# Bias rows in a box of their own, grouped queries read out before the merge, and layer 1's differential keys turned first, in a two-layer mixer trunk

## The chip, the cores and the metric

The kernel runs on one core of one Trainium2 chip. The metric is the device time of one execution in microseconds (us), the median of several runs. TensorE is called PE here, VectorE DVE, ScalarE ACT, GpSimd POOL and SyncE SP, as the profile does.

## The reference

Two layers act on 256 latent and 256 context tokens of width 1024. In each layer one normalised, modulated input h goes through four parallel mixers (a gated linear recurrence, differential attention, grouped-query attention, neighbourhood attention). Each mixer's output is multiplied by its own branch weight, scaled by a sigmoid gate and summed; then come an output projection and a feed-forward block. Context tokens go through the mixers of layer 0 only; in layer 1 they serve as keys and values. Cut to what this change touches:

```
(a_x, a_g, d_q, d_k, d_v, g_q, g_k, g_v, n_q, n_k, n_v, gates) = split_columns(h @ w_in + b_in)
y_b = rms_norm(softmax(q1 k1) v - lam * softmax(q2 k2) v)      # differential, 4 heads, rotary on q and k
y_c = gqa_attend(rope(rms_norm(g_q)), rope(rms_norm(g_k)), g_v)  # 4 query heads, 2 key heads
m = 0
for j, y in enumerate((y_a, y_b, y_c, y_d)):
    m = m + sigmoid(gates[j]) * (y @ w_branch[j])
out = m @ w_out + b_out
```

## The kernel before

Every matmul of full precision is three passes (`mm3`, L243 to L246): a weight tile is loaded by SP into one of two `raw` boxes (L185), ACT casts its high part `wh` (L214), DVE or POOL subtracts to get the low part `wl` (L217), and PE multiplies high by high, high by low, low by high. The passes accumulate in PSUM banks. The pool `mm` has three banks, `s` and `t` two each, `o` one.

`mixer` (L585) writes the work of a layer in this order: the recurrence (`lru`), the gates of branch 0, the differential branch up to its values (`diff` until its first `yield`), `merge(0)`, then differential attention and the gates of branch 1, then `gqa` until its first `yield`, `merge(1)`, the rest of `gqa` with the gates of branch 2, the start of `na`, `merge(2)`, and so on. A scheduler of the framework lays this program order out on the engines when the kernel is built: it may let independent work pass on each engine, and the order of each engine is then fixed. An engine runs its instructions in that order and waits where an operand is not there.

`merge(j)` (L660) takes the eight 128-wide slices of the model width in turn. For each slice PE does 6 matmuls of the branch output `y` with the branch weight into one `mm` bank, DVE multiplies the bank by the gate (`mt`, or `macc` for branch 0; L688), and for branches 1 and 2 POOL adds the product to `macc` (L691). In layer 0 a slice is 512 tokens wide, in layer 1 it is 256 wide.

`E` (L135) hands out six boxes of 128 x 516, shared by all short-lived tiles: the turned halves `dp` of the differential queries and keys, `dx` and `dt` beside them, the exponentials `e`, `mt`, the read-out queries `gx`, and the bias rows. `bias_row` (L578) takes such a box and asks for 256 bias values, spread over all 128 partitions, with a DMA on POOL's queue. It is called when the projection that needs it is written: in `v_proj` (L849) for the values of `diff` and `na`, and in `gqa` (L1047) for queries and for keys and values. DVE then reads the PSUM bank, adds the bias row and frees the bank (L856, L1064, L1084).

In `gqa` the query projection fills one `mm` bank for each segment: two in layer 0 (context and latent), one in layer 1 (`qs`). The banks are read out only after the `yield`, which is after `merge(1)`.

In `diff` (L946) queries and keys are turned one after the other: DVE takes the bank (`dx`, L964), PE permutes (`pp`, L967), DVE does the rotary products and the split into `dp` (L969 to L971, L829), and SP copies the halves in 24 small DMAs (L976) into `qx` or `qk`, the operands of the scores (`sps`, L1024). In layer 1 the key projection was done ahead: its two banks (one `mm`, one `o`) are full when the layer begins. There a query slice goes to `qx` and a key slice to `qk`; in layer 0 it is the other way round. A score of one head map needs the three DMAs of its query slice and the three of its key slice.

`par` (L482) is a pool of two boxes with a layer's small parameters; `params(0)` and `params(1)` take one each.

Of the kernel before, what the change touches and what calls it, by code (L numbers as in the profile page):

```python
# [8 lines left out]
F32 = mybir.dt.float32  # L9
# [101 lines left out]
class Trunk:  # L111
# [367 lines left out]

    def params(self, l, rowt):  # L480
        nc, i = self.nc, self.i
        par = self.per.tile([128, R_END], F32, tag="par", name="par", bufs=2)  # L482
# [93 lines left out]
    def bias_row(self, l, c0):  # L576
        t = self.E("brow2")[:, 0:256]
        self.nc.gpsimd.dma_start(t, self.i["b_in"][l:l + 1, c0:c0 + 256].broadcast_to([128, 256]))  # L578
        return t
# [5 lines left out]
    def mixer(self, l, x, hT, pool, tags):  # L585
# [6 lines left out]
        self.w = w  # L592
        self.full = [(0, T)] if l == 0 else [(0, 256), (256, 512)]
# [255 lines left out]
    def v_proj(self, col):  # L849
        nc = self.nc  # L850
        v = self.v_tiles()
        br = self.bias_row(self.l, col)
        units = self.cols_tm(self.w, col)
        for seg in range(2):
            ps = self.tm_chunk(units, seg)
            nc.vector.tensor_tensor(out=v[:, 2 * seg:2 * seg + 2, :], in0=ps, in1=bc(br, 1, [128, 2, 256]), op=ALU.add)  # L856
        return v
# [91 lines left out]
    def diff(self):  # L949
# [9 lines left out]
        for dst, col, slices, scale, order in ((q, "d_q", self.own, 32 ** -0.5, (0, 0, 1)),  # L959
                                               (k, "d_k", self.full, 1.0, (0, 1, 0))):  # L960
# [17 lines left out]
        v = self.v_proj(COL["d_v"])  # L978
# [69 lines left out]
    def gqa(self):  # L1048
# [4 lines left out]
        brq = self.bias_row(self.l, COL["g_q"])  # L1053
        uq = self.cols_tm(self.w, COL["g_q"])
        qs = []
        for seg in self.segs():
            qs.append(self.tm_chunk(uq, seg))
            if seg == self.segs()[0]:
                self.first_tm = self.last_tm
        yield  # L1060
        xs = []
        for ps in qs:
            t = view(self.E("gx"), 2, 256)
            nc.vector.tensor_tensor(out=t, in0=ps, in1=bc(brq, 1, [128, 2, 256]), op=ALU.add)  # L1064
            xs.append(view(t.rearrange("p a b -> p (a b)"), 2, 4, 64))
        normed = self.qk_norm(self.segs(), xs, 4, 0)
# [9 lines left out]
        brk = self.bias_row(self.l, COL["g_kv"])  # L1076
# [75 lines left out]
    def na(self):  # L1152
# [3 lines left out]
        q = [(qb[:, h, 0], qb[:, h, 1]) for h in range(4)]  # L1156
        for isk, col, slices, scale in ((0, "n_q", self.own, 0.125), (1, "n_k", self.full, 1.0)):
# [45 lines left out]
        v = self.v_proj(COL["n_v"])  # L1203
# [141 lines left out]
    def run(self):  # L1345
# [10 lines left out]
        self.l = 0  # L1356
# [212 lines left out]
```

## Time and profile before

| what | us |
|---|---|
| median of 3 runs (1497.87 to 1501.22) | 1499.52 |
| the profiled execution | 1494.38 |
| its span in the profile | 1492.6 |
| PE busy in the span | 1399.7 (94%) |
| DVE busy | 916.8 (61%) |
| ACT busy | 733.2 (49%) |
| POOL busy | 257.5 (17%) |

The profiled execution lies 5.1 us under the median, and 1.8 us of it lie around the span. Times in the text are us from the span's start. A row of the timeline has its start, its duration, the engine, the line, the operation, the tile written and the tiles read, the shape, the count, and in square brackets how long the engine was idle before and what released it. Matmuls overlap in the pipeline, so PE's pace is read from one start to the next (0.23 us for a 512-column pass at the full clock), not from the duration. Layer 0's mixers run from about 85 to 480 us, layer 1's from about 957 to 1245 us.

### The profile page before, as it was taken

Reading aid. Unit: us, or ns where it says so; the run is one execution under the profiler, and the core shown is the slowest. Engines: PE = TensorE matmul, PEld = TensorE weight load, DVE = VectorE, ACT = ScalarE, POOL = GpSimd, SP = SyncE. Lnnn points to the kernel's source line nnn. Section 1 sums busy time; section 2 is a strip of 40 time slices with the busy share of each in tenths; the row PEclk is TensorE's granted clock in tenths of the full one; section 3 lists DMA queues with packets and bytes.
Section 4 is the critical chain, followed back from the end, with each engine's and each line's share of the span. In section 5 each row is a group of like instructions: output and inputs, shape, how many; then the busy total and the mean of one; then the engine's idle time right before and its main releaser. Section 6 shows DMA issues by size and latency. Waiting matters only on the chain.

```text
span 1492.6 us, 22269 instructions
## 1 busy us (share of the span) xinstructions
PE 1399.7 (94%) x8420; PEld 1167.9 (78%) x8420; DVE 916.8 (61%) x1711; ACT 733.2 (49%) x1257; POOL 257.5 (17%) x445
## 2 busy tenths in 40 slices
PE   5999998899999999999999999998899999699997
PEld 3788676766887778777778888887788987599986
DVE  5664763642643988554545436767767657688856
ACT  4572452243254456454454223582636365577743
POOL 1120001211422102212222000010011321043421
PEclk9999999999999999999999999998899999799999
DMA  9425515213623454444543332343443526355562
GB/s 347 145 86 158 160 50 181 79 57 112 219 64 122 177 181 163 145 141 167 170 167 130 141 141 85 125 166 104 151 132 113 179 92 219 114 191 175 193 232 107
DMA packets 149310, 219.42 MB, mean 147 GB/s; under 512 B 10023, under 2 KB 118915, under 8 KB 149203
## 3 DMA queue, kind: packets, MB, share of 16 engines
q1 hardware_dynamic: 146690, 213.26, 42.8%
q0 software_dynamic: 2512, 4.73, 1.2%
q8 instruction: 67, 1.10, 0.3%
q14 instruction: 41, 0.33, 0.1%
HBM read 208.75 MB, written 1.08 MB: 141 GB/s over the span
## 4 chain that ended last, share of the span: by engine, by line
PE 76%; DVE 7%; DMA 6%; ACT 5%; issue 3%; SPq 2%; POOL 0%; DVEq 0%; ACTq 0%; POOLq 0%
PE mm L244 18%; PE mm L245 17%; PE mm L246 17%; PE acc L245 4%; PE acc L246 4%; PE acc L244 4%; PE ops L893 3%; PE adaps L380 2%; PE tp L885 2%; DMA raw<-in_w_in_dram 2%; DVE wl L217 2%; ACT wh L214 1%; DMA raw<-in_w_out_dram 1%; DMA raw<-in_ffn_w_dram 1%; PE sps L913 1%
## 5 line engine op out<-in xcount | busy, mean ns | idle before, releaser
L244 PE MATMUL mm<-hh,wh 128*128 128x256 f32 (+1 forms) x1488 | 501.7, 340 | 7.5 <-ACT gate L650 2.9
L245 PE MATMUL mm<-hl,wh 128*128 128x256 f32 (+1 forms) x1488 | 498.4, 336 | 0.0
L246 PE MATMUL mm<-hh,wl 128*128 128x256 f32 (+1 forms) x1488 | 497.3, 335 | 0.0
L214 ACT CAST wh<-raw 128x1024 fp32r<-128x1024 f32 x253 | 262.9, 1048 | 343.7 <-PE mm L245 155.1
L217 DVE TENSOR_TENSOR wl<-raw,wh 128x1024 fp32r<-128x1024 f32 x232 | 292.6, 1270 | 212.2 <-ACT wh L214 211.8
L244 PEld LDWEIGHTS mm<-hh,wh 128*128 128x128 f32 x1488 | 284.6, 192 | 46.8 <-issue 8.6
L246 PEld LDWEIGHTS mm<-hh,wl 128*128 128x128 f32 x1488 | 285.1, 192 | 31.1 <-issue 3.3
L245 PEld LDWEIGHTS mm<-hl,wh 128*128 128x128 f32 x1488 | 285.7, 192 | 29.4 <-issue 3.5
L1334 DVE SCALAR_TENSOR_TENSOR cv<-up,par,cv 128x512 f32<-128x512 f32 (+1 forms) x176 | 134.3, 764 | 52.7 <-ACT cv L1331 37.4
L245 PE MATMUL acc<-wl,a 128*128 128x512 f32 x232 | 90.7, 391 | 0.8 <-POOL wl L217 0.8
L870 ACT ACTIVATE e<-sps,nm 128x512 f32<-128x512 f32 (+1 forms) x96 | 59.2, 618 | 63.7 <-DVE nm L869 59.4
L246 PE MATMUL acc<-wh,a 128*128 128x512 f32 x232 | 90.3, 390 | 0.0
L244 PE MATMUL acc<-wh,a 128*128 128x512 f32 x232 | 89.6, 390 | 0.0
L869 DVE TENSOR_REDUCE nm<-sps 128x1 f32<-128x512 f32 (+1 forms) x96 | 56.7, 599 | 53.5 <-PE sps L914 37.4
L1338 POOL TENSOR_TENSOR cv<-cv 128x512 f32<-128x512 f32 (+1 forms) x44 | 50.0, 1135 | 165.9 <-ACT cv L1337 165.8
L244 PE MATMUL mm<-wh,hh 128*128 128x256 f32 x240 | 68.9, 287 | 0.8 <-DVE mt L688 0.8
L245 PE MATMUL mm<-wl,hh 128*128 128x256 f32 x240 | 68.2, 284 | 0.0
L246 PE MATMUL mm<-wh,hl 128*128 128x256 f32 x240 | 68.1, 284 | 0.0
L217 POOL TENSOR_TENSOR wl<-raw,wh 128x1024 fp32r<-128x1024 f32 x21 | 50.5, 2404 | 98.5 <-ACT wh L214 98.5
L312 ACT ACTIVATE junk<-x,nmu 128x512 bf16<-128x512 f32 x44 | 31.7, 721 | 70.0 <-DVE nmu L304 33.5
L1331 ACT ACTIVATE cv<-mm,cb,par 128x512 f32<-128x512 f32 (+1 forms) x88 | 58.5, 665 | 0.0
L244 PE MATMUL mm<-yh,wh 128*128 128x512 f32 (+1 forms) x128 | 47.0, 371 | 12.2 <-DVE mt L688 7.3
(313 smaller groups left out, 2135.8 us busy)
## 6 DMA issues: line engine op xcount, KB each, us to landing
raw<-in_ffn_w_dram SPq DMA_DIRECT2D x66, 1024.0 KB
raw<-in_w_in_dram SPq DMA_DIRECT2D x52, 1024.0 KB
raw<-in_w_ada_dram SPq DMA_DIRECT2D x40, 1024.0 KB
raw<-in_w_branch_dram SPq DMA_DIRECT2D x8, 1024.0 KB
raw<-in_w_out_dram SPq DMA_DIRECT2D x8, 1024.0 KB
w<-in_w_ada_dram SPq DMA_DIRECT2D x4, 1024.0 KB
w<-in_w_ada_dram SPq DMA_DIRECT2D x8, 512.0 KB
qk<-dp SPq DMA_DIRECT2D x48, 64.0 KB
```

The source lines that it names most:

```text
L214: nc.scalar.copy(hi, src)
L217: eng.tensor_tensor(out=lo, in0=src, in1=hi.bitcast(F32), op=ALU.subtract)
L244: nc.tensor.matmul(out, lhsT=lh, rhs=rh, start=start, stop=False)
L245: nc.tensor.matmul(out, lhsT=lh, rhs=rl, start=False, stop=False)
L246: return nc.tensor.matmul(out, lhsT=ll, rhs=rh, start=False, stop=stop)
L312: nc.scalar.activation(self.junk, halves[n], AF.Square, bias=nmu, accum_out=q[n])
L869: nc.vector.tensor_reduce(out=nm, in_=s if fold is None else fold, op=ALU.max, axis=AX.X, negate=True)
L870: nc.scalar.activation(e, s, AF.Exp, bias=nm, accum_out=total)
L893: self.last_pv = nc.tensor.matmul(o[64 * hh:64 * hh + 64, cs], lhsT=v[:, kt, vcol(hh)], rhs=pts[hh][:, kt, :], start=kt == 0, stop=kt == n ...
L1331: nc.scalar.activation(cv, view(ps, 2, 256)[:, 0:nseg, :], AF.Identity, bias=self.cb[:, j:j + 1], scale=tap[1])
L1334: nc.vector.scalar_tensor_tensor(out=cv, in0=up[:, :, k:k + 256], scalar=tap[k], in1=cv, op0=ALU.mult, op1=ALU.add)
L1338: nc.gpsimd.tensor_tensor(out=conv[0], in0=conv[0], in1=conv[1], op=ALU.mult)
```

## The change

Bias rows of `diff` and `na` values and of `gqa` keys and values no longer take an `E` box. A layer's mixer takes a `par` box of its own (`self.brow`), and the three rows are asked for, one after the other into the same box, as soon as `diff`, `gqa` or `na` begins. In layer 0 that box is the one that `params(1)` later uses (`self.boxes`); in layer 1 it is the box that `params(0)` had. The query row of `gqa` stays in an `E` box (`own=False`). In `gqa` the query banks are read out (`gx`) before the `yield`. In `diff` of layer 1 the keys are turned ahead of the queries.

```diff
     def params(self, l, rowt):
-        par = self.per.tile([128, R_END], F32, tag="par", name="par", bufs=2)
+        par = self.boxes.pop() if self.boxes else self.par_box()
...
-    def bias_row(self, l, c0):
-        t = self.E("brow2")[:, 0:256]
+    def bias_row(self, l, c0, own=True):
+
+        t = self.brow if own else self.E("brow2")[:, 0:256]
         self.nc.gpsimd.dma_start(t, self.i["b_in"][l:l + 1, c0:c0 + 256].broadcast_to([128, 256]))
         return t
...
+        box = self.par_box()
+        self.brow = box[:, 0:256]
+        if l == 0:
+            self.boxes.append(box)
...
-    def v_proj(self, col):
+    def v_proj(self, col, br):
         v = self.v_tiles()
-        br = self.bias_row(self.l, col)
...
-        for dst, col, slices, scale, order in ((q, "d_q", self.own, 32 ** -0.5, (0, 0, 1)),
-                                               (k, "d_k", self.full, 1.0, (0, 1, 0))):
+        br = self.bias_row(self.l, COL["d_v"])
+        sides = ((q, "d_q", self.own, 32 ** -0.5, (0, 0, 1)), (k, "d_k", self.full, 1.0, (0, 1, 0)))
+        for dst, col, slices, scale, order in sides[::-1] if self.l else sides:
...
-        brq = self.bias_row(self.l, COL["g_q"])
+        brq = self.bias_row(self.l, COL["g_q"], False)
+        brk = self.bias_row(self.l, COL["g_kv"])
         uq = self.cols_tm(self.w, COL["g_q"])
-        qs = []
+        xs = []
         for seg in self.segs():
-            qs.append(self.tm_chunk(uq, seg))
+            ps = self.tm_chunk(uq, seg)
             if seg == self.segs()[0]:
                 self.first_tm = self.last_tm
-        yield
-        xs = []
-        for ps in qs:
             t = view(self.E("gx"), 2, 256)
             nc.vector.tensor_tensor(out=t, in0=ps, in1=bc(brq, 1, [128, 2, 256]), op=ALU.add)
             xs.append(view(t.rearrange("p a b -> p (a b)"), 2, 4, 64))
+        yield
```

DVE in layer 0 around `merge(1)`, before the change (`do`, `yl` end the differential branch, `mt` is the merge, `gx` the query read-out, `gy` the start of the query norm):

```order
L996 COPY vt<-dn_2169 128x512
L217 TENSOR_TENSOR wl<-raw,wh 128x1024
L1003 SCALAR_TENSOR_TENSOR do<-vt,dlam,nb 128x512
L217 TENSOR_TENSOR wl<-raw,wh 128x1024
L829 TENSOR_TENSOR yl<-do,yh 128x512
L383 TENSOR_TENSOR ada<-ada,adaps 128x256
L688 SCALAR_TENSOR_TENSOR mt<-gate,mm 128x512 x8
L1064 TENSOR_TENSOR gx<-mm,brow_2187 128x512 x2
L217 TENSOR_TENSOR wl<-raw,wh 128x1024 x2
L1129 TENSOR_TENSOR gy<-gx,nw 128x512
```

The same place on DVE after the change:

```order
L1004 COPY vt<-dn_2169 128x512
L1070 TENSOR_TENSOR gx<-mm,brow_2187 128x512
L217 TENSOR_TENSOR wl<-raw,wh 128x1024
L1070 TENSOR_TENSOR gx<-mm,brow_2187 128x512
L1011 SCALAR_TENSOR_TENSOR do<-vt,dlam,nb 128x512
L217 TENSOR_TENSOR wl<-raw,wh 128x1024
L837 TENSOR_TENSOR yl<-do,yh 128x512
L383 TENSOR_TENSOR ada<-ada,adaps 128x256
L696 SCALAR_TENSOR_TENSOR mt<-gate,mm 128x512 x8
L217 TENSOR_TENSOR wl<-raw,wh 128x1024
L1135 TENSOR_TENSOR gy<-gx,nw 128x512
```

Both read-outs moved from behind the eight `mt` to ahead of `do` and `yl`; the norm still follows the merge.

SP in layer 1 around the differential copies, before the change (the five loads are of the recurrence's gate, branch 0's gates, and the differential projections; the single load behind the `w_ada` load is the first quarter of branch 1's gates):

```order
L185 DMA raw<-in_w_in_dram 128x8x256 x5
L185 DMA raw<-in_w_branch_dram 128x2x1024
L185 DMA raw<-in_w_ada_dram 128x2x1024
L185 DMA raw<-in_w_in_dram 128x8x256
L976 DMA qx<-dp 32x256 x24
L976 DMA qk<-dp 32x512 x24
L185 DMA raw<-in_w_in_dram 128x8x256 x4
```

The same place on SP after the change:

```order
L185 DMA raw<-in_w_in_dram 128x8x256 x5
L185 DMA raw<-in_w_branch_dram 128x2x1024
L185 DMA raw<-in_w_ada_dram 128x2x1024
L984 DMA qk<-dp 32x512 x24
L984 DMA qx<-dp 32x256 x24
L185 DMA raw<-in_w_in_dram 128x8x256 x5
```

The key copies stand ahead of the query copies, and the load of the first quarter of branch 1's gates stands behind all 48 copies.

PE in layer 1 at the end of `merge(0)` (`mm<-yh`), before the change (`mm<-hh` are the gates of branch 1, in passes of three matmuls; between the two scores stand 6 matmuls of the merge and 21 of the gates):

```order
L246 MATMUL mm<-yh,wl 128x256
L1024 MATMUL sps<-qk,qx 128x512
L244 MATMUL mm<-yh,wh 128x256
L245 MATMUL mm<-yl,wh 128x256
L246 MATMUL mm<-yh,wl 128x256
L244 MATMUL mm<-yh,wh 128x256
L245 MATMUL mm<-yl,wh 128x256
L246 MATMUL mm<-yh,wl 128x256
L244 MATMUL mm<-hh,wh 128x256
```

The same place on PE after the change (`tp` are transposes of the exponentials, `ops` the products with the values):

```order
L246 MATMUL mm<-yh,wl 128x256
L1032 MATMUL sps<-qk,qx 128x512 x4
L892 MATMUL tp<-cst,e 128x128 x4
L1032 MATMUL sps<-qk,qx 128x512 x3
L892 MATMUL tp<-cst,e 128x128 x4
L1032 MATMUL sps<-qk,qx 128x512 x2
L892 MATMUL tp<-cst,e 128x128 x4
L900 MATMUL ops<-vt 64x256
L1032 MATMUL sps<-qk,qx 128x512 x2
L892 MATMUL tp<-cst,e 128x128 x4
L1032 MATMUL sps<-qk,qx 128x512
L900 MATMUL ops<-vt 64x256 x7
```

Between the merge and the twelfth score no matmul of the gates is left; 48 of them stood there before.

## Rows read from the trace of the kernel before

**Rows 1.** The page, part 1: busy time, share of the span, instructions.
```profile
PE 1399.7 (94%) x8420; PEld 1167.9 (78%) x8420; DVE 916.8 (61%) x1711; ACT 733.2 (49%) x1257; POOL 257.5 (17%) x445
```
**Rows 2.** Stretches: PE, PEld, DVE, ACT, POOL busy, granted PE clock, DMA share, GB/s.
```profile
253.70:275.30 21.60, 14.76 (x67) 8.78 (x66) 8.65 (x14) 2.78 (x4) 8.98 (x7) 1.00 0.29 98
376.70:389.10 12.40, 12.40 (x67) 9.57 (x66) 9.20 (x12) 3.05 (x4) 7.95 (x7) 1.00 0.77 233
1028.00:1043.70 15.70, 11.30 (x53) 9.27 (x52) 10.22 (x21) 2.28 (x3) 0.62 (x1) 0.69 0.35 83
1043.70:1068.50 24.80, 20.29 (x101) 15.03 (x100) 17.50 (x34) 16.06 (x35) 0.00 (x0) 0.78 0.44 131
1068.50:1093.30 24.80, 23.68 (x186) 21.59 (x185) 14.83 (x35) 12.88 (x25) 0.55 (x1) 1.00 0.50 164
```
**Rows 3.** Waits in 253.7 to 275.3: engine, line, releaser, us in total, times, longest.
```profile
PE mm L244 <- DVE mt L688: 5.6, 7, 0.9
```
**Rows 4.** Timeline of PE in layer 0's merge(1): one slice ends, the next begins.
```profile
256.93 0.40 PE L246 MATMUL mm<-yh,wl 128*128 128x512 f32 x1
258.11 0.50 PE L244 MATMUL mm<-yh,wh 128*128 128x512 f32 x1 [0.78 <-DVE mt L688]
```
**Rows 5.** Timeline of DVE at that merge's end: the last product, the read-outs.
```profile
274.61 0.69 DVE L688 SCALAR_TENSOR_TENSOR mt<-gate,mm 128x512 f32<-128x512 f32 x1 [1.82 <-PE mm L246]
275.21 1.28 DVE L1064 TENSOR_TENSOR gx<-mm,brow 128x512 f32<-128x512 f32 x2
```
**Rows 6.** Timeline of POOL: seven additions of layer 0's merge(2).
```profile
382.79 9.77 POOL L691 TENSOR_TENSOR macc<-macc,mt 128x512 f32<-128x512 f32 x7 [1.35 <-DVE mt L688]
```
**Rows 7.** Timeline of PE in layer 0's merge(0): a score waits for its copies.
```profile
151.13 0.36 PE L1024 MATMUL sps<-qx,qk 96*128 96x256 f32 x1 [1.78 <-DMA qx<-dp]
```
**Rows 8.** Timeline of SP in layer 0: key copies, then the next loads.
```profile
144.42 15.09 SPq L976 DMA_DIRECT2D qx<-dp  x24
159.60 1.18 SPq L185 DMA_DIRECT2D raw<-in_w_in_dram  x2
```
**Rows 9.** Timeline of POOL and DVE in layer 1's merge(0): the bias row and its readers.
```profile
1037.65 0.62 POOL L578 DMA_DIRECT2D brow<-in_b_in_dram  x1 [20.03 <-DVE macc L688]
...
1041.42 1.29 DVE L856 TENSOR_TENSOR vt<-mm,brow 128x512 f32<-128x512 f32 x2 [1.71 <-DMA brow<-in_b_in_dram]
```
**Rows 10.** Timeline of SP in layer 1: query copies, key copies, the loads behind them.
```profile
1020.09 15.66 SPq L976 DMA_DIRECT2D qx<-dp  x24
1035.86 15.32 SPq L976 DMA_DIRECT2D qk<-dp  x24
1051.28 1.18 SPq L185 DMA_DIRECT2D raw<-in_w_in_dram  x2
```
**Rows 11.** Timeline of DVE in layer 1, up to the first query half.
```profile
1016.95 0.96 DVE L813 SCALAR_TENSOR_TENSOR ge<-ge,lru 128x256 f32<-128x256 f32 x1
...
1018.83 0.41 DVE L815 TENSOR_TENSOR yl<-ge,yh 128x256 fp32r<-128x256 f32 x1
...
1020.05 0.42 DVE L829 TENSOR_TENSOR dp<-dx,dp 128x256 fp32r<-128x256 f32 x1
```
**Rows 12.** Timeline of PE in layer 1: scores, gate matmuls at either clock, the first products.
```profile
1041.21 0.63 PE L1024 MATMUL sps<-qk,qx 96*128 96x512 f32 x1
...
1046.45 0.41 PE L245 MATMUL mm<-hl,wh 128*128 128x256 f32 x1
1046.66 0.41 PE L246 MATMUL mm<-hh,wl 128*128 128x256 f32 x1
...
1050.28 0.28 PE L245 MATMUL mm<-hl,wh 128*128 128x256 f32 x1
1050.40 0.28 PE L246 MATMUL mm<-hh,wl 128*128 128x256 f32 x1
...
1051.60 0.63 PE L1024 MATMUL sps<-qk,qx 96*128 96x512 f32 x2
...
1065.20 3.34 PE L893 MATMUL ops<-vt 128*64 128x256 f32 x14
```

More of the change, by code (lines that the diff above doesn't have):

```diff
@@ L478, in setup, with par_box @@
         nc.scalar.activation(self.silu_c[:, :, 0:2], pc[:, 0:16].rearrange("p (s k) -> p k s", s=2), AF.Silu)
+    def par_box(self):
+        return self.per.tile([128, R_END], F32, tag="par", name="par", bufs=2)
     def params(self, l, rowt):
         nc, i = self.nc, self.i
-        par = self.per.tile([128, R_END], F32, tag="par", name="par", bufs=2)
+        par = self.boxes.pop() if self.boxes else self.par_box()
         q = nc.sync
@@ L977, in diff @@
                                           parts[order[r]][32 * g:32 * g + 32, ts].bitcast(F32))
-        v = self.v_proj(COL["d_v"])
+        v = self.v_proj(COL["d_v"], br)
         yield
@@ L1075, in gqa @@
         kb = view(self.X("gkk", F32R), 2, T)
-        brk = self.bias_row(self.l, COL["g_kv"])
         uk = self.cols_tm(self.w, COL["g_kv"])
@@ L1156, in na @@
         q = [(qb[:, h, 0], qb[:, h, 1]) for h in range(4)]
+        br = self.bias_row(self.l, COL["n_v"])
         for isk, col, slices, scale in ((0, "n_q", self.own, 0.125), (1, "n_k", self.full, 1.0)):
@@ L1202, in na @@
         prepare(0)
-        v = self.v_proj(COL["n_v"])
+        v = self.v_proj(COL["n_v"], br)
         if self.l:
@@ L1355, in run @@
                 x[seg].append(xt)
-        self.l = 0
+        self.l, self.boxes = 0, []
         self.pre, self.w = {}, i["w_in"][0]
```

## The prediction

> **What bounds the kernel now.** I read the page first, for the engine that has no slack: PE is busy 94% of the span, the next engine 61% [rows 1]. So an edit pays only where PE stands still or runs at its lower clock, and a microsecond taken out of such a place comes off the end, unless something behind it is late for another reason. Next I read each `merge` as a stretch, with PE's busy time, count and granted clock beside it, because the change aims at the three PSUM banks of `mm` that a merge shares with unread projections [rows 2]. Three places stand out.
>
> In layer 0, `merge(1)` takes 21.60 us with PE busy 14.76. `merge(2)` does the same 67 matmuls in 12.40 us, busy all the time, at the same clock 1.00 [rows 2]. The list of waits names the reason: PE waits seven times, 5.6 us in all, for DVE's `mt` [rows 3]. The timeline shows one such step: the last pass of a slice starts at 256.93, the next slice only at 258.11, after 0.78 of waiting [rows 4]. The two query banks are read at 275.21, behind the last `mt` at 274.61 [rows 5]. Until then the merge has one bank in place of three, and PE and DVE take turns.
>
> In layer 0, `merge(0)` has a wait of 1.78, but for a copy into `qx` and not for a bias row [rows 7]. In layer 1, `merge(0)` takes 15.70 us with PE busy 11.30 at a clock of 0.69 [rows 2]; POOL's bias request waits 20.03 for an `E` box, and the value banks are read at 1041.42, once it has landed [rows 9]. What stands behind it is the start of differential attention, fed by SP's copies.
>
> **Grouped queries read out early, layer 0.** What is removed is the bank shortage. The upper end is the difference to `merge(2)`: 21.60 - 12.40 = 9.2. The lower end is the listed waits alone, 5.6. I take the upper end first, because the rest of the difference (busy 14.76 against 12.40) is the pipeline filling again after each wait: the pass after it starts later than 0.23 apart from its neighbour. What is added: the two read-outs, 1.28 of DVE together [rows 5], stand ahead of `do` and `yl`, which the merge's second pass needs. A cover for one of them is likely, since a weight split stands between the two and the banks are full early; I charge 0.7, with 0 and 1.28 as ends. So 9.2 - 0.7 = **8.5 gained**, ends 5.6 - 1.28 = 4.3 and 9.2.
>
> Are DVE, POOL and the boxes fast enough for a slice in 12.40 / 8 = 1.55? DVE needs 0.69 per `mt` [rows 5]. POOL did seven additions in 9.77, 1.40 each [rows 6]. An `mt` box is held 0.69 + 1.40 = 2.1, so two boxes are enough; the `gx` tiles hold two of the six during the merge, four are left for `mt` and others. `merge(2)` runs with the same three engines and shows that it goes. Behind the merge the key-value projection, the query norm and the key norm begin where the last `mt` ends, on both kernels; they move forward with it and keep their own waits. The request for key-value bias no longer needs an `E` box, which may give back a little more there; nothing in the sum counts it.
>
> **Bias row, layer 0.** SP's order is unchanged there: the 24 `qx` copies end at 144.42 + 15.09 = 159.5, the loads of the next gates follow at 159.60 [rows 8]. An earlier bias row lets PE do merge matmuls before the scores rather than between them, and the gates behind are still as late as their loads. I take **0**. Ends: a gain of 1.78 if the wait of rows 7 vanishes, a loss of 1.55 if one merge slice is put ahead of scores that were ready.
>
> **Keys first and bias row, layer 1.** PE's part of `merge(0)` is 48 passes of 256 columns. At the full clock two such starts lie 0.12 apart, at the half clock 0.21 [rows 12]; 48 x 0.12 = 5.8. With the value banks read at once the merge should end about 8 us earlier, at 1036. That gain is not the branch's gain. Attention waits for 48 copies on SP, 15.66 + 15.32 in one row [rows 10], and the first batch starts when its first half is split on DVE, at 1020.05. Ahead of the first key half now stand two `ge` and two `yl` fewer (the starts of rows 11 lie 0.33 apart, one `ge` takes 0.88): 0.88 + 3 x 0.33 = 1.9, less some 0.2 for wider key operations. So both batches move **1.7 earlier**: the second from 1035.86 to 1034.1, the last copy from 1051.2 to 1049.5.
>
> Between the first score, 1041.21, and the fourth, 1051.60 [rows 12], there stood merge and gate matmuls, partly at the half clock. Now the scores stand one behind the other, limited by copies: the first some 5.4 us behind the second batch's start, as before (1041.21 - 1035.86), so at 1039.5; three copies of 0.65 for the next head map, 2 us, and waits of the exponentials put the fourth at 1042 to 1045, say 1044. The first products end 1068.5 - 1051.6 = 16.9 behind the fourth score [rows 2, 12]: 1061, which is 7.5 earlier. But the 48 gate matmuls that PE used as filling are still to do, and their first load is now asked for behind all copies, at 1049.6, where before it went ahead. From 1061 there follow the 24.8 us of the last stretch in rows 2 and 48 x 0.12 = 5.8 more: 1091.6, against 1093.3. **Gain 1.5.** Ends: 7.5 if the 48 find idle places on PE before 1061; a loss of 5.8 if attention comes no earlier and the filling is only moved.
>
> The trace shows PE half-clocked in just such places: 0.21 between starts at 1046.45, a clock of 0.69 in `merge(0)` and 0.78 behind it [rows 2, 12]. If the 48 gate matmuls all ran so, they would cost 48 x 0.09 = 4.3 more. (The Trainium skill, "TensorE: Matmul & The Clock Gate", section "HAM oscillation — how this bites in real kernels", speaks against this part of the change: a PE that idles for data between bursts drops to half its clock, and the next burst begins there. The rows agree; by it alone the layer's 1.5 gain would become a loss of 2.8.)
>
> **The rest.** `merge(1)` of layer 1 has one query segment, so two banks stay free either way, and the neighbourhood rows come earlier to a place where PE did not wait for them: 0 for both. The extra `par` boxes are memory, not time.
>
> Sum on the profiled execution: -8.5 + 0 - 1.5 = -10, so 1494.4 becomes 1484.4. That execution is 5.1 under the median; the same -10 on the median 1499.5 gives **1489.5**.
>
> **The rivals.**
>
> *Both merges pay in full.* Layer 1 gives its upper end, as PE's idle places between scores take the gate matmuls after all: -8.5 - 7.5 = -16, 1483.5. For it: PE is the bound and 4.4 us of the merge are idle. Against: the load behind the copies.
>
> *Layer 1's attention is starved.* Half clock alone: -8.5 - 1.5 + 4.3 = -5.7, 1493.8. Attention no earlier: -8.5 + 5.8 = -2.7, 1496.8. Both: +1.6, 1501. I take 1496.8. For it: the order with no filling between merge and twelfth score, and the clock rows. Against: key halves ready 1.7 earlier.
>
> *The copies slip: slower.* The wider key halves hold `E` boxes until their copies have landed. If the next half finds no box, SP stands for a landing and a turning: a landing took 1041.42 - 1038.27 = 3.1 on POOL's queue [rows 9], a turning from the last `ge` takes at least 1020.05 - 1016.95 = 3.1 [rows 11], together 6.2. Two such gaps among the four halves cost 12.4, three 18.6, and scores and gate load are late by as much. From a slip of 10 the kernel is slower than before; two gaps give -10 + 12.4 = +2.4, three +8.6; middle +5.5, **1505**. Against: in the kernel before the two batches lie 0.1 apart with the same six boxes [rows 10], and a bias row no longer takes one.
>
> *The merge keeps its cadence.* If `gx` and what else is in `E` leave `mt` one box, a slice takes 2.1 and a hand-over, some 2.2 in place of 2.4: 8 x 0.25 = 2 gained, with layer 1 -3.5, **1496**; with nothing gained 1498. Against: `merge(2)`, above.
>
> **How the numbers follow.** A measurement of this kernel can tell about 0.2%, 3 us, from no change. Forecast, 1486 to 1493.5: 0.52. Both in full, about 1483.5: 0.14. Starved attention, about 1496.8: 0.16, half of it within 0.2%. Copies slip, about 1505: 0.10, of it 0.08 slower and 0.02 within. Cadence kept, 1496 to 1498: 0.08, nearly all within. Faster: 0.52 + 0.14 + 0.08 + 0.01 = 0.75; within: 0.08 + 0.02 + 0.07 = 0.17; slower 0.08. The range 1482.5 to 1497.5 leaves out the slip, the far end of starvation and a corner of the full pay, about 0.18.
>
> **What would show it.** Layer 0's `merge(1)` should last 12 to 13.5 us, with PE's waits for `mt` gone and both `gx` ahead of the first `mt`; if the waits stay, the first step is wrong. The key-value projection should begin about 8.5 earlier and that lead should hold at layer 0's end. Scores of layer 0's differential branch should stand within 1.5 us of their old place. In layer 1, less the lead, SP should copy keys from about 1018.4 without gaps to 1049.5; `merge(0)` should last about 8 us; the fourth score should come near 1044, the first products near 1061, and the gates end at 1091.6. A PE that stands waiting with half clock beyond 1061, or SP with gaps between the batches, would make the layer's term wrong; a `merge(1)` of over 17 us would take the forecast out of its range.

## The result and the profile after

The changed kernel takes 1476.36 us (median of 4 runs, 1474.13 to 1479.34) against 1498.69 for the kernel before, measured beside it (4 runs, 1496.59 to 1501.22): a ratio of 0.985, 95% interval 0.9825 to 0.9875. That is 22 us, with 19 to 26 inside the interval. 1489.5 was predicted, a gain of 10, with a range that ended at 1482.5. The direction was right, the size less than half of what came. In the profiled executions the last instructions stand 20.3 us earlier.

Part 1 of the page after, with the columns of [rows 1]:

```profile
PE 1395.8 (95%) x8420; PEld 1166.2 (79%) x8420; DVE 917.3 (62%) x1711; ACT 731.9 (50%) x1257; POOL 259.5 (18%) x445
```

The counts are unchanged, so no work has gone. PE is busy 3.9 us less for the same 8420 matmuls; the other 16 us are time in which it stood still. To see where, I took stretches between the same landmarks of PE in both traces: from the first matmul of layer 0's `merge(1)` to that of its `merge(2)`, and from the end of layer 0's feed-forward block to the first matmul of layer 1's `merge(1)`. The columns are those of [rows 2]: the stretch, its length, busy time and count of PE, PEld, DVE, ACT and POOL, the granted clock (the share of the full clock that TensorE was given, 0.5 or 1.0 at any moment), DMA share and GB/s. Before:

```profile
253.80:376.80 123.00, 112.58 (x605) 84.74 (x605) 59.30 (x123) 44.01 (x88) 21.68 (x28) 0.97 0.29 99
932.00:1099.10 167.10, 149.64 (x1103) 134.05 (x1102) 115.93 (x241) 95.55 (x167) 10.16 (x11) 0.93 0.43 137
```

After:

```profile
256.00:366.90 110.90, 108.28 (x606) 83.86 (x605) 60.12 (x122) 43.60 (x87) 22.44 (x28) 0.98 0.33 110
921.50:1079.80 158.30, 146.00 (x1103) 130.28 (x1101) 115.27 (x241) 95.08 (x167) 11.35 (x11) 0.94 0.45 144
```

Below I call them **stretch A** (layer 0, grouped queries) and **stretch B** (layer 1, differential branch). A gives 12.1 us, B 8.8. The rest of the span loses 0.6: a start-up that was 1.9 longer in this execution, where nothing is changed, less 1.3 in small pieces. So both places are those of the prediction; A was forecast at 8.5, B at 1.5.

Inside A, `merge(1)`, the stretch that answers to the first line of [rows 2]:

```profile
256.00:268.40 12.40, 12.40 (x67) 9.39 (x66) 8.24 (x13) 1.72 (x3) 6.87 (x6) 1.00 0.51 170
```

It is as long as `merge(2)` was to the tenth, with PE busy throughout; the seven waits of [rows 3] are gone. DVE's timeline at its beginning (start, duration, engine, line, operation, tiles, shape, count, idle time before):

```profile
249.66 0.69 DVE L1070 TENSOR_TENSOR gx<-mm,brow 128x512 f32<-128x512 f32 x1 [2.90 <-PE mm L246]
...
256.20 0.68 DVE L1070 TENSOR_TENSOR gx<-mm,brow 128x512 f32<-128x512 f32 x1
...
258.60 0.69 DVE L837 TENSOR_TENSOR yl<-do,yh 128x512 fp32r<-128x512 f32 x1
...
260.75 1.88 DVE L696 SCALAR_TENSOR_TENSOR mt<-gate,mm 128x512 f32<-128x512 f32 x3 [1.14 <-PE mm L246]
```

One read-out fell into a pause of DVE, the other stands ahead of `do` and `yl` as foreseen. PE didn't wait for the `yl` at 258.60, because its order puts the high passes of three slices together there, which three banks allow:

```profile
259.40 0.85 PE L244 MATMUL mm<-yh,wh 128*128 128x512 f32 x3
260.09 0.40 PE L245 MATMUL mm<-yl,wh 128*128 128x512 f32 x1
```

Inside B, `merge(0)`, then the stretch up to the end of the first products (of the exponentials with the values, `ops`), then the gates of branch 1:

```profile
1016.20:1023.10 6.90, 6.90 (x52) 6.38 (x51) 6.17 (x17) 0.81 (x2) 0.62 (x1) 1.00 0.42 107
1023.10:1044.10 21.00, 15.47 (x45) 8.18 (x44) 15.65 (x34) 12.83 (x30) 0.00 (x0) 0.59 0.44 135
1044.10:1074.00 29.90, 29.90 (x242) 28.14 (x241) 20.06 (x39) 17.96 (x33) 0.55 (x1) 1.00 0.56 181
```

`merge(0)` takes 6.9 in place of 15.7, at clock 1.00 in place of 0.69. Behind it PE starves: 45 matmuls in 21 us, clock 0.59. Then it works without a gap for 29.9 us at 1.00. SP's copies and the load behind them, as in [rows 10]:

```profile
1004.58 15.56 SPq L984 DMA_DIRECT2D qk<-dp  x24
1020.32 15.94 SPq L984 DMA_DIRECT2D qx<-dp  x24
1036.30 13.63 SPq L185 DMA_DIRECT2D raw<-in_w_in_dram  x4
```

Counted from the begin of B, copies start at 83.1 in place of 88.1 and end at 114.7 in place of 119.2: 5.0 and 4.5 earlier, not 1.7.

### The profile page after: what moved, and what is told of

Same layout as the page of the kernel before. It is cut to its first block, busy times and chain, and to the rows that moved or that the text cites. A ratio compares the mean times of both kernels' runs of the same rounds, so it can differ in the third digit from the quotient of the medians.

```text
span 1472.3 us, 22271 instructions
## 1 busy us (share of the span) xinstructions
PE 1395.8 (95%) x8420; PEld 1166.2 (79%) x8420; DVE 917.3 (62%) x1711; ACT 731.9 (50%) x1257; POOL 259.5 (18%) x445
## 4 chain that ended last, share of the span: by engine, by line
PE 76%; DVE 8%; DMA 6%; ACT 5%; issue 3%; SPq 1%; POOL 0%; DVEq 0%; ACTq 0%; POOLq 0%
PE mm L244 18%; PE mm L245 17%; PE mm L246 17%; PE acc L245 4%; PE acc L246 4%; PE acc L244 4%; PE ops L900 3%; PE adaps L380 2%; PE tp L892 2%; DMA raw<-in_w_in_dram 2%; DVE wl L217 2%; ACT wh L214 1%; DMA raw<-in_w_ada_dram 1%; DMA raw<-in_ffn_w_dram 1%; PE sps L920 1%
## 5 line engine op out<-in xcount | busy, mean ns | idle before, releaser
L245 PEld LDWEIGHTS mm<-hl,wh 128*128 128x128 f32 x1488 | 285.1, 192 | 29.9 <-issue 4.0
L699 POOL TENSOR_TENSOR macc<-macc,mt 128x512 f32<-128x512 f32 (+1 forms) x32 | 36.1, 1159 | 104.6 <-DVE mt L696 104.6
```

Source lines behind the costliest of these rows:

```text
L245: nc.tensor.matmul(out, lhsT=lh, rhs=rl, start=False, stop=False)
L699: nc.gpsimd.tensor_tensor(out=self.macc[n], in0=self.macc[n], in1=dst, op=ALU.add)
```

## Experiments

Each kernel was timed beside the kernel before; ratios are to that, with 95% intervals, and can differ by some tenths of a per cent from the quotient of the medians. A and B vary by some 1 us between two profiles: the changed kernel, profiled twice, showed 110.9 and 109.5 for A, 158.3 and 158.5 for B. B holds the same matmuls, by tile and shape, in all versions. Other stretches vary more, as the end of this document says.

### The read-out alone

```diff
-        qs = []
+        xs = []
         for seg in self.segs():
-            qs.append(self.tm_chunk(uq, seg))
+            ps = self.tm_chunk(uq, seg)
...
-        yield
-        xs = []
-        for ps in qs:
             t = view(self.E("gx"), 2, 256)
...
             xs.append(view(t.rearrange("p a b -> p (a b)"), 2, 4, 64))
+        yield
```

> The kernel before with one part of the change: the grouped queries' banks are read out ahead of merge(1); bias rows stay in E, layer 1 turns queries first. Theory 1 (the bank shortage is all of layer 0's gain): layer 0's merge(1) falls from 21.6 to 12.4-13 us, the lead behind layer 0's mixers is the 12 us that the full change shows there (median about -12, 1487). Rival (the read-out gives only the merge, and the 3 us behind it come from the key-value bias row in its own box): merge(1) as above, but the lead at layer 0's end is 8 to 9 (median 1490 to 1491). Layer 1 as before in both, its merge(0) 15.7 us.

Measured: 0.9922 (0.9892 to 0.9953), median 1484.56. Stretches A and B:

```profile
253.30:365.30 112.00, 108.36 (x606) 83.87 (x605) 60.23 (x122) 43.45 (x87) 22.44 (x28) 0.98 0.33 109
922.10:1089.50 167.40, 149.30 (x1103) 133.43 (x1102) 116.22 (x241) 94.94 (x167) 10.25 (x11) 0.93 0.43 136
```

A loses 11.0 of its 123.0 by this part alone, B nothing (167.4 against 167.1). Theory 1 holds in the main: the bank shortage is layer 0's gain. All kernels with the read-out have 109.5 to 112.2 in A, all without it 121.9 to 123.0. The two with the read-out and the key-value row still in `E` are the longest, 112.0 and 112.2, the eight profiles with the box 109.5 to 111.1, so the rival's share is about 1 us. PE's waits in A behind the merge show it: without the box PE waits three times before the scores (1.9, 0.6 and 1.2 here), with it twice (1.4 and 1.2).

### Keys first alone, and the box alone

The first has these lines of the change and nothing else:

```diff
-        for dst, col, slices, scale, order in ((q, "d_q", self.own, 32 ** -0.5, (0, 0, 1)),
-                                               (k, "d_k", self.full, 1.0, (0, 1, 0))):
+        sides = ((q, "d_q", self.own, 32 ** -0.5, (0, 0, 1)), (k, "d_k", self.full, 1.0, (0, 1, 0)))
+        for dst, col, slices, scale, order in sides[::-1] if self.l else sides:
```

The second has everything except those lines and the read-out, that is, of the change:

```diff
+        box = self.par_box()
+        self.brow = box[:, 0:256]
...
-        t = self.E("brow2")[:, 0:256]
+        t = self.brow if own else self.E("brow2")[:, 0:256]
...
+        br = self.bias_row(self.l, COL["d_v"])
...
+        brk = self.bias_row(self.l, COL["g_kv"])
...
+        br = self.bias_row(self.l, COL["n_v"])
```

> The kernel before with one part of the change: layer 1 turns the differential keys first; bias rows in E, query banks read out behind the merge. Theory 1 (layer 1's gain comes from the copies: keys lie ready in their banks, so the first turn needn't wait for the layer's own query projection): SP's copies start about 5 us earlier against the layer's start, and most of the 8.8 us of layer 1 is gained by this part alone, 6 to 8 us (median about 1492). Rival (layer 1's gain comes from the value banks, read at once): the copies start earlier, but merge(0) stays at 12 us or more, the scores stand behind it, and the gain is 0 to 2 us (median 1497 to 1499).

> The kernel before with one part of the change: bias rows of values, and of grouped keys and values, in their own box and asked for when the branch begins; the query banks are read out behind merge(1), layer 1 turns queries first. Theory 1 (copies decide in layer 1): layer 1's merge(0) falls from 15.7 to about 8 us, the scores come no earlier since the copies end as before, and layer 1 gains 0 to 2; layer 0 gains 0 to 1, so the median is about 1497 to 1499. Rival (value banks decide): layer 1 gains 6 to 8 by this part alone, median 1490 to 1493. If the bias row gives layer 0 the 3 us behind merge(1), another 3 less.

Measured, keys first: 0.9961 (0.9939 to 0.9983), median 1489.5 of ten runs from 1487.22 to 1496.09; stretch B, its `merge(0)`, and the request for the value row:

```profile
928.40:1089.10 160.70, 144.06 (x1102) 129.87 (x1101) 115.41 (x241) 94.50 (x167) 11.35 (x11) 0.96 0.44 142
1029.20:1039.00 9.80, 7.37 (x53) 6.32 (x51) 5.79 (x13) 1.92 (x5) 0.62 (x1) 1.00 0.28 67
```

```profile
1030.35 0.62 POOL L578 DMA_DIRECT2D brow<-in_b_in_dram  x1 [15.58 <-DVE dp L829]
```

Measured, the box: 0.9934 (0.9914 to 0.9953), median 1486.88; stretch B, its `merge(0)`, SP in its layer 1, and the fourth score on PE:

```profile
933.20:1094.20 161.00, 144.78 (x1103) 129.54 (x1102) 116.56 (x241) 95.55 (x167) 10.15 (x11) 0.96 0.44 142
1029.20:1040.40 11.20, 7.79 (x54) 6.64 (x53) 9.66 (x21) 2.29 (x3) 0.62 (x1) 1.00 0.26 65
```

```profile
1021.40 15.20 SPq L984 DMA_DIRECT2D qx<-dp  x24
1036.71 16.66 SPq L984 DMA_DIRECT2D qk<-dp  x24
```

```profile
1046.61 0.39 PE L1032 MATMUL sps<-qk,qx 96*128 96x512 f32 x1
```

Either part alone shortens B, by 6.4 and by 6.1; together they give 8.8, so for a good part they remove the same loss. With keys first the value row still takes an `E` box, but it is asked for 1.1 us behind the begin of `merge(0)`, against 9.7 before the change [rows 9], and both parts alone have `merge(0)` at a clock of 1.00, against 0.69. Keys first alone gives the 6 to 8 that the theory of the copies named for it, but since its value row comes earlier as well, that run doesn't part copies from banks.

The box does. It meets its rival, that the value banks decide, and not the 0 to 2 of the copies: its copies end 120.2 us behind the begin of B (1036.71 + 16.66 - 933.2), 1.0 *later* than before, and yet its fourth score comes 6.2 earlier (113.4 against 119.6) and B is 6.1 shorter. So the copies' end didn't set B's end. Of those 6.1, 4.9 are busy time, with the same 1103 matmuls: PE ran longer at the full clock (0.96 in place of 0.93). The other 1.2 are waits.

### The change without keys first

Against the changed kernel:

```diff
-        sides = ((q, "d_q", self.own, 32 ** -0.5, (0, 0, 1)), (k, "d_k", self.full, 1.0, (0, 1, 0)))
-        for dst, col, slices, scale, order in sides[::-1] if self.l else sides:
+        for dst, col, slices, scale, order in ((q, "d_q", self.own, 32 ** -0.5, (0, 0, 1)),
+                                               (k, "d_k", self.full, 1.0, (0, 1, 0))):
```

> The changed kernel with layer 1's keys turned behind its queries again, as before the change; the other two parts stay. Theory 1 (copies decide in layer 1): layer 0 keeps its 12 us, layer 1 keeps 0 to 2 of its 8.8, so the median is 1485 to 1487 and the copies start where they did. Rival (value banks decide in layer 1): the median is within 2 us of the changed kernel, 1477 to 1479.

Measured: 0.9864 (0.9832 to 0.9896), median 1475.93; stretch B:

```profile
922.40:1082.30 159.90, 143.67 (x1103) 129.11 (x1101) 115.71 (x241) 95.04 (x167) 10.15 (x11) 0.97 0.45 143
```

The rival holds: it is as fast as the changed kernel (1476.36, and 1474.15 when it was measured again, below). Keys first gives at most 1.6 in B when the box is there, and nothing that the medians show.

### One row

Only layer 1's differential value row leaves `E`:

```diff
+        if l:
+            self.brow = self.per.tile([128, R_END], F32, tag="par", name="par", bufs=2)[:, 0:256]
...
+        br = self.bias_row(self.l, COL["d_v"], True) if self.l else None
...
-        v = self.v_proj(COL["d_v"])
+        v = self.v_proj(COL["d_v"], br)
```

> The kernel before with a single row moved: layer 1's differential value bias gets its own box and is asked for when diff begins; every other row stays in E, queries first, read-outs behind the merge. The bias box alone gained 9 us in layer 1 though the copies ended no earlier. Theory A (in the kernel before the scores stood in PE's order behind merge(0), which that one row held up): this row alone gives layer 1's 6 us at merge(1)'s start, its merge(0) lasts about 11 us, the fourth score comes about 6 earlier against the layer's start while the copies end as before; median about 7 below the kernel before. Theory B (the rows of gqa and na in layer 1, or a freer E in general, give the gain): merge(0) is shorter but merge(1) starts within 2 us of before, and the median is within 3 of it. Theory C (the copies decide, as the prediction had it): 0 to 2.

Measured: 0.9949 (0.9922 to 0.9976), median 1491.77 (1481.54 to 1497.72; its profile is of the slowest). Stretch B, and SP:

```profile
935.80:1098.70 162.90, 146.55 (x1103) 132.07 (x1102) 116.53 (x241) 95.31 (x167) 9.62 (x10) 0.95 0.44 139
```

```profile
1025.16 15.20 SPq L979 DMA_DIRECT2D qx<-dp  x24
1040.46 15.78 SPq L979 DMA_DIRECT2D qk<-dp  x24
```

The copies end at 120.4, 1.2 later than before, and B is 4.2 shorter: theory A in kind, though short of its size (4.2 of 6, `merge(0)` 13.0 us and not 11, the fourth score 3.1 earlier and not 6, median 4 lower and not 7). The 9 us that its text gives the box are of the median; in B the box gave 6.1. Theories B and C, both with at most 2 to 3 us, are out by the profile, and a second pair says the same: the kernel below with this row and the read-out has 163.5 in B, the read-out alone 167.4. By the times alone (4 between the medians, 3.6 to 11.7 by the ratio's interval) C is out and B just. What the whole box has above this row is 1.9 in B here, and 3.6 in the pair with the read-out (159.9 against 163.5); which of the other rows it comes from stays open.

B is not the whole time. In this profile and in that of keys first, the next stretch, from layer 1's `merge(1)` to its `merge(2)`, was 4.6 us longer than before the change, with the same matmuls at a clock of 0.93 in place of 1.00. Before, keys first, and one row:

```profile
1099.10:1165.80 66.70, 62.56 (x487) 57.45 (x485) 45.27 (x95) 32.98 (x60) 11.89 (x17) 1.00 0.35 114
1089.10:1160.40 71.30, 66.40 (x486) 61.15 (x485) 45.27 (x95) 33.06 (x60) 11.90 (x17) 0.93 0.33 107
1098.70:1170.00 71.30, 66.46 (x485) 61.17 (x485) 45.26 (x95) 33.12 (x60) 11.91 (x17) 0.93 0.33 107
```

All other profiles have 64.9 to 68.1 there. So in these two executions most or all of B's gain was lost again behind it. Whether that belongs to the two versions or to some of their executions, whose times spread by 9 and 16 us, isn't shown.

### Copies on a second queue

Three kernels put part of layer 1's copies on GpSimd's queue: the queries' (keys first), the keys' (queries first; the condition reads `col == "d_k"`), and what is called every second copy below: the three copies of every second slice (keys first; `self.l and g % 2`). The first:

```diff
                     for r in range(3):
-                        nc.sync.dma_start(
+                        (nc.gpsimd if self.l and col == "d_q" else nc.sync).dma_start(
...
```

> The changed kernel with layer 1's 24 query copies on GpSimd's queue in place of SP's, so that the loads of branch 1's gates no longer stand behind them and PE has gate matmuls between the scores. Theory A (in the changed kernel the early copies lead into a stretch of 21 us in which PE has nothing but scores, at a clock of 0.59, and the 48 gate matmuls behind it give back about 6): layer 1 gains 4 to 6 more, median 1470 to 1472, the stretch between merge(0) and the first pair's products at a clock near 1. Rival (attention's own chain over ACT and DVE sets the end, the filling is free either way): within 2 of the changed kernel. Third case (copies on GpSimd's queue cost more than on SP's 0.65 each): first products later, median above 1478.

Measured: 0.9852 (0.9819 to 0.9885), median 1475.65. Stretch B, its part around the scores, and the end of the first products on PE:

```profile
924.20:1081.90 157.70, 141.65 (x1103) 129.15 (x1102) 115.33 (x241) 95.50 (x167) 23.22 (x35) 0.97 0.46 145
```

```profile
1035.30:1058.20 22.90, 21.35 (x156) 18.38 (x156) 20.28 (x36) 17.79 (x38) 0.62 (x2) 1.00 0.50 167
```

```profile
1056.24 1.94 PE L900 MATMUL ops<-vt 128*64 128x256 f32 x14
```

This is the run that says most. The starved stretch is gone: 156 matmuls in 22.9 us at clock 1.00 around the scores, where the changed kernel had 45 in 21.0 at 0.59. The first products end at 134.0 from B's begin (1058.2 - 924.2), 11.4 later than in the changed kernel (1044.1 - 921.5 = 122.6). And B is as long as there, 157.7 against 158.3. So the end doesn't follow the first products, on which the prediction's layer 1 term was built: what gate work stands ahead of them needn't be done behind them. Theory A's mechanism is seen (busy time falls by 4.4), but its gain of 4 to 6 isn't: PE, being faster, waits 3.8 more (157.7 - 141.65 = 16.05 against 12.3), with one wait of 4.5 for the gates' first weights. In its number the rival came, within 2 us of the changed kernel; its reason, the chain over ACT and DVE, wasn't tested.

> The changed kernel with queries turned first again, and layer 1's 24 key copies, the second batch, on GpSimd's queue, so that the two batches no longer share SP. If SP's 48 copies in a row limited attention (the prediction's step), the first products come 4 to 7 earlier than with queries first and one queue, median 1469 to 1472. If the scores stand behind PE's order and the softmax, and the copies are early enough, the median stays within 2 of that version's 1476, and scores come no earlier.

Measured: 0.9896 (0.9859 to 0.9933), median 1483.96; stretch B, and the last of its key copies on GpSimd:

```profile
917.90:1084.50 166.60, 146.44 (x1103) 132.59 (x1102) 115.55 (x241) 95.39 (x167) 22.05 (x35) 0.95 0.44 137
```

```profile
1035.31 0.50 POOL L984 DMA_DIRECT2D qk<-dp  x1 [0.33 <-DMA qk<-dp]
```

Here the copies end at 117.9, no later than on one queue (before: 119.2), but the scheduler interleaves scores and gates in another order: 61 gate matmuls stand ahead of the first score, where the version with queries first and one queue has 18. The first score comes at 1036.32, 118.4 behind B's begin, and no score in this trace waits for a copy. B is 6.7 longer than with queries first and one queue. Neither expectation was met: the median was 8 us above that version's, by the ratios 5, with intervals that overlap. As far as the trace shows, the loss in B comes with the order; no run has this order without GpSimd's copies.

> The changed kernel with every second copy of layer 1 (12 of each batch) on GpSimd's queue. Theory A (filling for PE between the scores is what is missing in the changed kernel): as with the queries on GpSimd's queue, 4 to 6 gained over the changed kernel, median 1470 to 1472. Theory of the copies: both batches end in half the time, first products 6 to 8 earlier than in the changed kernel, median 1468 or below. If the copies on GpSimd cost more than on SP, no gain.

Measured: 0.9813 (0.978 to 0.9845), median 1470.19; stretch B:

```profile
920.30:1077.50 157.20, 141.12 (x1103) 128.85 (x1101) 114.81 (x241) 95.36 (x167) 23.19 (x35) 0.98 0.45 145
```

The clock rises to 0.98 and busy time falls by 4.9, but idle time is 16.1 against 12.3, so B gains 1.1 only. The first products end at 1053.7, 133.4 behind B's begin: 10.8 later than in the changed kernel and not 6 to 8 earlier, so the theory of the copies is out. Theory A's median came, its 4 to 6 in layer 1 didn't: the median is 4 to 6 below the changed kernel's; the profile of B explains 1 of them.

### The two places alone, and the copies in other arrangements

The first of these has the read-out and the one row, by the two diffs above. The second has every second copy of both layers on GpSimd (`if g % 2`), the third every second copy of layer 1 with queries first. The last is the changed kernel as their yardstick, with no edit.

> The kernel before with two things changed: layer 1's differential value bias in its own box, asked for when diff begins, and the grouped queries read out ahead of the merge. The runs so far put 11 to 13 us on the read-out (layer 0) and 4 to 6 on that row (layer 1, by PE's half clock and its idle time up to merge(1), not by the copies). Theory 1 (these two are the change): ratio to the kernel before 0.986 to 0.990, 15 to 21 us, PE's stretch from layer 1's start to merge(1) 160 to 163 us in place of 167. Rival (the other rows or the key order carry part of it): a ratio of 0.991 or above.

> The changed kernel with every second copy of both layers on GpSimd's queue. Theory A (PE's half clock and idle time while the next gates' load stands behind copies is what is left to gain in either layer): layer 1 gains as with its half alone, about 5; layer 0, where PE stood for loads behind the copies at 157 to 170, gains 2 to 4 more; ratio to the kernel before 0.977 to 0.980. Rival (layer 0's loads are early enough): as the changed kernel with layer 1's half alone, 0.981. Third case (GpSimd's copies delay its weight splits and gate products in layer 0): 0.983 or above.

> The changed kernel with queries first again and every second copy of layer 1 on GpSimd's queue. If the order of keys and queries matters only through what fills PE between scores, this is as fast as keys first with half the copies on GpSimd (ratio 0.980 to 0.983). If keys first brings a gain of its own once the copies are no longer one queue (its copies start 4 to 5 us earlier), this is 3 to 5 us slower than that version (0.984 or above).

> The changed kernel itself on the same chip as these three, as their yardstick: a ratio to the kernel before of 0.983 to 0.988. Half the copies on GpSimd's queue in both layers should be 5 to 9 us faster than this, the row and the read-out alone 0 to 5 us slower.

Measured side by side on one chip:

| kernel | ratio to before | interval | median (range) | stretch B |
|---|---|---|---|---|
| one row and read-out | 0.9886 | 0.9864 to 0.9909 | 1481.48 (1478.56 to 1484.94) | 163.5 |
| every second copy, both layers | 0.9808 | 0.9786 to 0.9829 | 1470.41 (1468.3 to 1472.51) | 157.8 |
| every second copy, queries first | 0.9843 | 0.9822 to 0.9864 | 1474.85 (1473.73 to 1475.85) | 160.5 |
| the changed kernel | 0.9842 | 0.9821 to 0.9864 | 1474.15 (1473.97 to 1476.75) | 158.5 |

The row and the read-out carry 17 of the change's 22 to 24 us. Theory 1 of that run came in its ratio, with B just outside its 160 to 163; but the two are not the whole change, which has 7 us more (5 had been expected at most), 5.0 of them in B and 2.7 in A. Copies on two queues in layer 0 bring nothing more than in layer 1 alone (1470.41 against 1470.19): the rival holds. The stretch from 109 to `merge(1)` is 146.4 there, 145.4 before the change, although its gate loads no longer stand behind the copies:

```profile
109.20:255.60 146.40, 137.56 (x794) 107.97 (x793) 84.10 (x173) 57.47 (x118) 17.03 (x33) 0.98 0.44 136
```

Every second copy on GpSimd with keys first is the fastest version found. With both layers' copies split it lies 3.7 us below the changed kernel beside it, where 5 to 9 were expected, with no overlap of the runs, though the intervals of the ratios touch. With queries first the same arrangement gains nothing over the changed kernel. So the order of keys and queries matters once copies go out on two queues, by 4 us of median (against the version with both layers split) and about 3 in B. Of the two cases that were named for this run, the second came.

## Why the prediction was wrong

**What bounds the kernel**: right. PE is the bound, the two merges are where it stands, and the gain is PE's time idle and at half clock.

**Grouped queries, layer 0: -8.5; measured -12.1, mis-sized.** The merge itself went from 21.6 to 12.4, the upper end that the step named; the charge of 0.7 for the read-outs didn't fall due. The step that failed is the sentence that the work behind the merge moves forward and keeps its own waits. It gave 2.9 more (12.1 - 9.2). Of this 0.9 are waits: the three before the first scores were 0.47, 1.86 and 1.20 and are now 1.41 and 1.20. They go with the key-value row, since the two read-out kernels without the box still have all three. The other 2 are busy time of PE for the same work behind the merge, at a clock of 0.98 for all of A in place of 0.97, and that varies: A's repeat ran at 1.00 and took 109.5.

**Bias row, layer 0: 0.** Right: 145.4 before from 108.4 to `merge(1)`, after the change 145.7, and 147.2 in its second profile.

**Layer 1's differential branch: -1.5; measured -8.8. This is the step that broke the range.** The prediction said that `merge(0)` would end about 8 us earlier; against B's begin it was 10.3 (111.9 before, 101.6 after). And then: "That gain is not the branch's gain. Attention waits for 48 copies on SP". Three runs contradict that sentence. With one row moved, and with the box, the copies end 1.0 to 1.2 later and B is 4.2 and 6.1 shorter. With the queries on GpSimd the first products come 11.4 later than in the changed kernel and B doesn't lengthen. The trace of the kernel before could have said it. These are PE's longest waits from `merge(0)` to the gates' end (1028 to 1093.3: engine, line, releaser, us in total, times, longest):

```profile
PE mm L244 <- DVE macc L688: 3.2, 5, 0.8
PE sps L1024 <- ACT e L870: 2.7, 4, 1.4
PE tp L885 <- DVE e L1033: 1.8, 3, 0.8
```

None of its waits there is put down to a copy. The fourth score, which starts at 1051.60, 0.4 behind the last copy [rows 10, 12], doesn't wait at all: in PE's order it follows on the end of `merge(0)`, 48 gate matmuls and two scores. That it stood so near the copies' end was chance; with the box it comes 6.8 ahead of that end (113.4 against 120.2). It stood behind `merge(0)`, which the value row held up in part, as the one row shows. In the changed kernel two scores do wait for query copies, 2.3 in all.

B's length is by definition PE's busy time plus its idle time, and since the matmuls are the same, busy time changes with the clock and with how closely they follow one another. Before, that was 149.6 busy and 17.5 idle; the row alone makes it 146.6 and 16.3, the box 144.8 and 16.2, keys first 144.1 and 16.6, the whole change 146.0 and 12.3. So each part alone took away mostly busy time, with less time at half clock; the whole change took 3.6 of busy time and 5.2 of waits, since its starved stretch is again at half clock. The prediction had that cost in front of it, a clock of 0.69 in `merge(0)` and 0.78 behind it [rows 2], and used it only as a price for what might come, not as a cost that the change could remove. By the pace of [rows 12], 48 matmuls at 0.21 in place of 0.12 are 4.3 more, an estimate; the merge's 48 and the 48 gate matmuls both ran so in part.

In the terms of the prediction's own sum, the term that was mis-sized is the first products, 7.5 earlier: they came 13.9 earlier (122.6 against 136.5). From these to the gates' end 30.6 was right (29.9, with PE busy throughout), and 13.9 less the 5.1 by which that is longer than before is the whole 8.8. (The working gives 1.7 where the prediction writes 1.5; that is of no weight.) Within the term, the copies were to start 1.7 earlier, measured 5.0, and the fourth score was to come 9.9 behind the second batch's start, measured 7.7. But the copies' lead is not what the layer lives on: with queries first, box and read-out, where it is gone, B is only 1.6 longer. The turning of keys needs no projection of the layer itself, since their banks are full; the first `dx` stands at 988.33, 66.8 behind B's begin, where before the first one was that of the queries, at 1013.27, 81.3 behind it. My count of DVE instructions ahead of the first half missed this, because an instruction that stands earlier in the order is worth more than its duration if what it waits for is there.

**The rivals.** "Both merges pay in full" was nearest with 1483.5 and had 0.14, but that was luck in layer 1: its reason, that PE's idle places between scores take the gate matmuls, did not come. In the changed kernel no gate matmul stands between `merge(0)` and the twelfth score, and PE idles there. It gave layer 1 7.5 where 8.8 came, and layer 0 8.5 where 12.1 came. "Starved attention" was right as a picture, PE at 0.59 for 21 us, and wrong as a price: B lost nothing by it against the versions with queries first. The rule of the Trainium skill ("TensorE: Matmul & The Clock Gate", "HAM oscillation — how this bites in real kernels"), half the clock for a PE that idles between bursts, agrees with that stretch (0.59); but the gate matmuls behind it ran at 1.00 from their beginning (1044.10 to 1074.00), and the loss of 2.8 that I worked out by it did not come. The copies didn't slip (1020.32 follows on 1004.58 + 15.56 within 0.2), and the merge didn't keep its cadence.

**What stays open**: which of the box's other rows gives its 2 to 4 us in B, and why the medians with every second copy on GpSimd lie some 4 to 6 lower where B shows 1. One pair of profiles can't say: that version's ended 4.3 us before the changed kernel's, and 3.5 of it was there before A begins (252.5 against 256.0), where nothing is changed. From B's end to the end of layer 1's output projection, stretches of 166 to 175 us were seen, 170.8 and 167.5 for the changed kernel alone. Between these two PE's waits agree to 0.1; the difference goes with the clock, 0.97 against 1.00 up to `merge(2)` and 0.94 against 1.00 in the output projection, and what brings that about isn't shown.

## What to carry to other kernels

Where one engine is busy for nearly the whole span, cost a stretch by that engine's account (work at full clock, idle time, time at half clock), and take a transfer's arrival for a limit only where the trace shows the engine waiting for it; here, before the change, the scores that came near the copies' end didn't wait for them. Put a half-clocked stretch into the sum beside its waits, as a cost that may go with them. It may also come back as idle time: with the queries on GpSimd, 4.4 of busy time less became 3.8 of waits more. And two edits that remove the same loss don't add up: test each alone and one without the other.

## What was not expected of the hardware

GpSimd's queue issued a copy in 0.50 us (eight in 3.97), SP's in 0.65 (24 in 15.56). GpSimd with the 24 query copies:

```profile
1021.01 3.97 POOL L984 DMA_DIRECT2D qx<-dp  x8 [1.16 <-ACT dp L836]
...
1028.89 2.02 POOL L984 DMA_DIRECT2D qx<-dp  x4 [1.41 <-DMA qx<-dp]
```

But it paused behind its own earlier copies, 1.41 here, which SP's rows, 24 copies without a break, don't show. The 24 query copies took 14.9 us from first to last (1021.01 to 1035.92), against 15.9 on SP.
